# Weight splits, norm vectors and product order in the mixers of a two-block transformer kernel

## The chip, the core and the metric

One core of one Trainium2 chip runs the whole program. Its engines, as the profile names them: PE (TensorE, matmul; PEld is its weight load), DVE (VectorE), ACT (ScalarE), POOL (GpSimd) and SP (SyncE), which issues the DMAs. The metric is device microseconds of one execution, as the median of several runs. Times in a trace count from the first instruction of the span.

## What is computed

Input x is 256 tokens of 1024 channels in float32. A first block (an even layer with two kinds of attention, an odd layer with retention, a final norm) is followed by a second block, and the change is in the first half of that second block, the mixers. Cut to that half:

```python
def first_block(x, ...):          # even_layer, odd_layer, then:
    return rms_norm(x, final_norm)

def second_block(h, ...):
    hn = rms_norm_2(h, g_pre_mix)
    u, q, k, v = split(hn @ w_in)                     # 512, 512, 128, 128 columns
    y_ssm = s5_mixer(u, ...)                          # state space, gelu, gated product with w_glu
    y_attn = sliding_window_sink_attention(rotary(q), rotary(k), v, sinks)   # 8 heads, window 128
    merged = concat([rms_norm_2(y_ssm, g_ssm_out), rms_norm_2(y_attn, g_attn_out)])
    h = h + rms_norm_2(merged @ w_out, g_post_mix)
    hn = rms_norm_2(h, g_pre_ffn)
    ff = (silu(hn @ w_gate) * (hn @ w_up)) @ w_down
    return h + rms_norm_2(ff, g_post_ffn)
```

## The kernel before

Tokens lie in two tiles of 128 partitions, `x[0]` and `x[1]`. Large products are made in float32r out of two parts of each operand: high part times high part, high times low and low times high (`mm_xs`, `proj_xs`, `proj_tmajor`, lines 268 to 336). The class `Weights` (lines 46 to 90) streams the weights: `load` (L63) issues a DMA of 512 KB on SP into one of five raw buffers; `_prepare` makes the high part with a cast on ACT (L73) and the low part with a subtraction (L78), on DVE or, for one tile in `SH[part]`, on POOL. The list at L36 gives the mixers one tile in 2 and the feed-forward one in 8. `next` prepares two tiles ahead of use, in six buffers. The mixers have 22 tiles of [128, 1024]: u 4, q 4, kv 2, glu 4, output 8.

The order of instructions on each engine is fixed when the program is built: a planner simulates the engines and takes what is ready first; `tc.high_priority()` moves a block ahead of others, and a manual dependency (`hold`, `behind`) puts one instruction behind another. At run time each engine takes its list in order, and SP its list of DMAs.

The stages of the mixers and what the change touches in them:

- Norms (L812 to L839): x times (g_pre_mix times g_final) on DVE (L224), then transposed on PE (L235), copied by ACT (L242) and subtracted by DVE (L243) into the two parts of xT. The factors of a token come in after the products: POOL multiplies x by g_final (L827), ACT squares (L202), DVE scales x (L837).
- u, q and kv products (`proj_xs`), each scaled by ACT on its way out of PSUM (L863, L876, L889; v by DVE, L890). The rotary embedding of q and k: six small POOL operations per call (L847 to L852); k is then doubled by DVE (L892) and transposed (L895).
- State space (L900 to L940): two halves `b`, each of two quarters `hf`. A quarter is 16 products with its tables into PSUM (L912), then on DVE two multiplications (L918, L919), two sums (L920, L921), two scans (L924), a multiplication by the cosines (L927) beside one by the sines on POOL (L928), two sums into X (L930, L931), and 12 products into bank `py` (L934 to L936), 64 columns wide: quarter 0 fills the partitions 0 to 63 of the bank, quarter 1 the others. Each is two PE records. Then a gelu on ACT (L938), transposes (L946) and a split (L326, L327).
- The tables of quarters 1 and 3 are loaded into buffers that earlier quarters used (L796, L797): the y table of a later quarter waits for an earlier quarter's products.
- Attention (L966 to L990): in pairs of heads, scores (L338), masked minimum (L346, L348), minimum with the sink (L970), exponentials on ACT (L355, L356, L973), the sum and its reciprocal (L974, L976), scaling (L977, L978), transposes (L362), copies (L364), p times v (L372) into the one `py` bank, squares (L985, added up on POOL, L987), and the two parts with the gain (L988, L989).
- POOL also makes x times g_pre_ffn (L993) and g_pre_ffn times g_post_mix (L994).
- The gated product of the state space (`zp`): DVE adds the biases (L1004, L1006), ACT the tanh, POOL multiplies by g_ssm_out (L1007), DVE makes the gated value (L1008), transposed into its two parts, and the same without the gain (L1010) for the norm's factor.
- Output: first the products of the state space's half (scaled by ACT, L1047), then those of attention's half; DVE joins them (L1064), ACT squares, DVE multiplies by the two gains (L1069) and adds x (L1074); transposes; POOL multiplies by g_post_mix (L1078) and DVE updates x (L1079). Then the feed-forward's first products start.

The line of the split before:

```python
i = nc.scalar.copy(h[:, :n], r[:, :n])                                                            # L73
self.lows.append(eng.tensor_tensor(lo[:, :n], r[:, :n], h[:, :n].bitcast(F32), op=ALU.subtract))  # L78
```

## Time and profile before

| | us |
|---|---|
| median of 3 runs | 811.92 |
| lowest, highest | 810.0, 812.02 |
| span of the profiled execution | 810.7 |
| PE busy | 780.7 (96%) |
| DVE busy | 560.7 (69%) |
| ACT busy | 408.3 (50%) |
| POOL busy | 237.2 (29%) |

The span runs from the first to the last instruction of one execution; the median of the runs is 1.2 us above it. A busy time is the union of an engine's instructions. PE's instructions overlap, so a row of PE can be busy without being at its peak rate. In a timeline a row gives start, duration, engine, line, operation, the tiles it writes and reads, the shape, how many were merged, and in brackets how long the engine was idle before it and what ended that.

### The profile page before, as it was taken

To read this page: it belongs to the slowest core of one execution; us is meant where nothing else is said; L and a number is where in the kernel's file an instruction comes from. 1 tells how busy PE (TensorE), PEld (TensorE's weight loads), DVE (VectorE), ACT (ScalarE), POOL (GpSimd) and SP (SyncE) were. 2 spreads that over 40 slices of the span, in tenths; PEclk is the share of its full clock that TensorE was granted. 3 is DMA by queue.
4 is the path that set the end of the run, shared out by engine and by line. 5 is a ranking of instruction groups with operands and counts; after the bars stand their busy time and mean duration, and the time that the engine had idled before them with its cause. 6 is when DMAs were issued, how large, how long until landed. Compare 5 with 4: busy or idle time off the path is not lost.

```text
span 810.7 us, 13533 instructions
## 1 busy us (share of the span) xinstructions
PE 780.7 (96%) x5114; PEld 682.1 (84%) x5114; DVE 560.7 (69%) x1013; ACT 408.3 (50%) x680; POOL 237.2 (29%) x274
## 2 busy tenths in 40 slices
PE   7989999999999999999999999989798999999996
PEld 5978997998997789898989887876577999999886
DVE  6987668678778468585766757698849856565433
ACT  5766565457455355344444355736645544443331
POOL 4662111013604212120202006853653322221110
PEclk9999999999999999999999999999999999999999
DMA  7687544644744757453636494852243765555431
GB/s 284 222 270 234 172 165 131 208 150 154 238 161 133 234 186 254 154 188 124 208 119 194 151 334 152 301 195 85 81 127 110 235 200 177 189 183 181 156 130 53
DMA packets 47427, 146.46 MB, mean 181 GB/s; under 512 B 5361, under 2 KB 11777, under 8 KB 47362
## 3 DMA queue, kind: packets, MB, share of 16 engines
q1 hardware_dynamic: 47362, 145.60, 54.5%
q8 instruction: 40, 0.66, 0.3%
q14 instruction: 25, 0.20, 0.1%
HBM read 137.70 MB, written 7.88 MB: 180 GB/s over the span
## 4 chain that ended last, share of the span: by engine, by line
PE 82%; DVE 5%; POOL 4%; issue 3%; ACT 3%; DMA 3%; SPq 0%; POOLq 0%; DVEq 0%; ACTq 0%
PE bpp L274 12%; PE bpp L275 12%; PE bpp L278 12%; PE bpp L251 9%; PE bpp L250 9%; PE bpp L252 9%; PE bat L252 3%; PE bat L251 3%; PE bat L250 3%; PE bpy L372 2%; PE bat L338 2%; PE bpt L362 1%; PE bpp L289 1%; DVE wl L78 1%; POOL wl L78 1%
## 5 line engine op out<-in xcount | busy, mean ns | idle before, releaser
L78 DVE TENSOR_TENSOR wl<-wraw,wh 128x1024 fp32r<-128x1024 f32 x211 | 276.5, 1321 | 114.9 <-ACT wh L73 114.9
L73 ACT CAST wh<-wraw 128x1024 fp32r<-128x1024 f32 (+1 forms) x233 | 238.6, 1045 | 190.0 <-PE bpp L251 54.1
L251 PE MATMUL bpp<-xTl,wh 128*128 128x256 f32 (+1 forms) x680 | 193.3, 284 | 0.0
L250 PE MATMUL bpp<-xTh,wh 128*128 128x256 f32 (+1 forms) x680 | 193.1, 284 | 0.0
L252 PE MATMUL bpp<-xTh,wl 128*128 128x256 f32 (+1 forms) x680 | 192.9, 284 | 0.0
L251 PEld LDWEIGHTS bpp<-xTl,wh 128*128 128x128 f32 (+1 forms) x680 | 127.3, 187 | 2.6 <-issue 1.9
L250 PEld LDWEIGHTS bpp<-xTh,wh 128*128 128x128 f32 (+1 forms) x680 | 127.3, 187 | 1.8 <-issue 1.3
L252 PEld LDWEIGHTS bpp<-xTh,wl 128*128 128x128 f32 (+1 forms) x680 | 127.3, 187 | 1.0 <-issue 0.8
L274 PE MATMUL bpp<-wh,xTh 128*128 128x512 f32 (+1 forms) x288 | 110.9, 391 | 0.8 <-ACT xTh L242 0.8
L275 PE MATMUL bpp<-wl,xTh 128*128 128x512 f32 (+1 forms) x288 | 109.6, 385 | 0.0
L78 POOL TENSOR_TENSOR wl<-wraw,wh 128x1024 fp32r<-128x1024 f32 x22 | 57.7, 2624 | 62.9 <-ACT wh L73 62.9
L278 PE MATMUL bpp<-wh,xTl 128*128 128x512 f32 (+1 forms) x288 | 74.2, 382 | 0.0
L274 PEld LDWEIGHTS bpp<-wh,xTh 128*128 128x128 f32 x288 | 54.5, 190 | 13.3 <-ACT xTh L242 1.7
L275 PEld LDWEIGHTS bpp<-wl,xTh 128*128 128x128 f32 x288 | 54.5, 189 | 11.1 <-DVE wl L78 0.6
L278 PEld LDWEIGHTS bpp<-wh,xTl 128*128 128x128 f32 x288 | 52.2, 188 | 11.1
L274 PE MATMUL bpp<-wh,yh 128*128 128x512 f32 x128 | 50.5, 400 | 0.0
L275 PE MATMUL bpp<-wl,yh 128*128 128x512 f32 x128 | 50.4, 396 | 0.0
L252 PE MATMUL bat<-xTh,wl 128*128 128x256 f32 x160 | 45.1, 282 | 0.0
L250 PE MATMUL bat<-xTh,wh 128*128 128x256 f32 x160 | 45.1, 282 | 0.0
L251 PE MATMUL bat<-xTl,wh 128*128 128x256 f32 x160 | 45.0, 281 | 0.0
L1119 POOL TENSOR_TENSOR gr<-gr,Rh 128x512 f32<-128x512 f32 x10 | 14.3, 1427 | 75.5 <-ACT th L1118 75.5
L278 PE MATMUL bpp<-wh,yl 128*128 128x512 f32 x128 | 35.6, 395 | 0.0
(380 smaller groups left out, 1312.3 us busy)
## 6 DMA issues: line engine op xcount, KB each, us to landing
wraw<-in_w_o SPq DMA_DIRECT2D x40, 512.0 KB, 4.3
wraw<-in_w_gate SPq DMA_DIRECT2D x22, 512.0 KB, 3.8
wraw<-in_w_up SPq DMA_DIRECT2D x22, 512.0 KB, 4.2
wraw<-in_w_dn SPq DMA_DIRECT2D x22, 512.0 KB, 3.7
wraw<-in_w_v SPq DMA_DIRECT2D x16, 512.0 KB, 4.6
wraw<-in_w_g SPq DMA_DIRECT2D x16, 512.0 KB, 4.4
wraw<-in_w_q SPq DMA_DIRECT2D x12, 512.0 KB, 4.1
wraw<-in_w_va SPq DMA_DIRECT2D x8, 512.0 KB, 6.6
```

The source lines that it names most:

```text
L73: i = nc.scalar.copy(h[:, :n], r[:, :n])
L78: self.lows.append(eng.tensor_tensor(lo[:, :n], r[:, :n], h[:, :n].bitcast(F32), op=ALU.subtract))
L250: T.matmul(ps, lh, rh, start=first, stop=False)
L251: T.matmul(ps, lh, rl, start=False, stop=False)
L252: T.matmul(ps, ll, rh, start=False, stop=last)
L274: T.matmul(ps, lh[:, k0 + k, st], wh, start=first and k == 0, stop=False)
L275: T.matmul(ps, lh[:, k0 + k, st], wl, start=False, stop=False)
L278: T.matmul(ps, ll[:, k0 + k, st], wh, start=False, stop=last and k == n - 1)
L289: m = T.matmul(ps[t], xp[:, k, st], tiles[k // 2][0][:, 512 * (k % 2):512 * (k % 2) + 512], start=xp is xTh and k == 0, stop=False)
L338: i = T.matmul(ps[j][:, o], q[rows, qs], k[rows, ks], start=True, stop=True)
L372: i = T.matmul(o[64 * j:64 * j + 64], v[:, b, vc], src, start=b == 0, stop=b == 1)
L1119: G.tensor_tensor(two(gr), two(gr), rep2(Rh), op=ALU.mult)
```

## The change

- No large operation of the mixers on POOL: `SH[2]` goes from 2 to 0, so DVE makes all 22 low parts; the sine product of the state space goes to DVE; the products by g_final, g_ssm_out, g_pre_ffn and g_post_mix leave POOL.
- Norm vectors in the weights: w_u3, w_q3, w_kv3 and w_o3 are multiplied by the norm's gain while they are split. A tile is then split in 2 blocks of 512 columns (kv: 4 of 256), each with an ACT activation scaled by a column of gains and a DVE `scalar_tensor_tensor`. Three small DMAs on SP bring the gains at the start of the program, in program order after the load of x[0] and ahead of the first weights.
- x is transposed without a gain; x is scaled by both factors in one DVE operation.
- The products into `py` are issued in pairs, one of each quarter, for both quarters after their X.
- The rotary embedding takes three POOL operations per call, k is doubled by ACT's broadcast read, v is scaled by ACT; the sink goes into the masked minimum as its starting value.
- The weights of attention's output half are planned, and its products made, before those of the state space's half.
- After the output products DVE multiplies by g_post_mix, updates x, then multiplies by g_pre_ffn.

```diff
-SH = (0, 0, 2, 8)
+SH = (0, 0, 0, 8)
...
+        g = self.gains[len(self.done)]
+        if g is not None:
+            m = g.shape[1]
+            for b in range(m):
+                sl = slice(b * n // m, (b + 1) * n // m)
+                i = nc.scalar.activation(h[:, sl], r[:, sl], AF.Copy, scale=g[:, b:b + 1])
+                if self.after:
+                    self.tc.add_manual_dep(i.ins, self.after[0].ins.name, NOSYNC, reason="order")
+                self.lows.append(nc.vector.scalar_tensor_tensor(lo[:, sl], r[:, sl], g[:, b:b + 1], h[:, sl].bitcast(F32),
+                                                                op0=ALU.mult, op1=ALU.subtract))
...
+    def gain_cols(name):
+        g = const.tile([P, 8], F32, name="gc_" + name)
+        nc.sync.dma_start(g, a[name])
+        return g
+
+    g_pm, g_fc, g_mo = (gain_cols(n) for n in ("g_pre_mix", "final_cols", "g_mix_out"))
+    V.tensor_tensor(g_pm, g_pm, g_fc, op=ALU.mult)
     for n in ("w_u3", "w_q3", "w_kv3"):
-        w.plan(xs(n, 0), SH[2])
+        w.plan(xs(n, 0), SH[2], g_pm)
...
-    for sl in (slice(0, 2), slice(2, 4)):
+    for i in (1, 0):
         for c in range(2):
-            w.plan(xs("w_o3", c)[sl], SH[2])
+            w.plan(xs("w_o3", c)[2 * i:2 * i + 2], SH[2], g_mo[:, 4 * i:4 * i + 4])
...
-        G.tensor_tensor(g_pm, g_pm, g_fin, op=ALU.mult)
-        last = [gained_transposed(t, halves(g_pm), KB[t]) for t in range(2)]
+        last = [transposed([x[t][:, :512], x[t][:, 512:]], 8, xTh, xTl, 0, t, KB[t]) for t in range(2)]
...
-            G.tensor_tensor(xc, xc, g_fin[:, h * 512:(h + 1) * 512], op=ALU.mult)
...
+        V.scalar_tensor_tensor(x[t], x[t], r1, g_fin, op0=ALU.mult, op1=ALU.mult)
...
-            A.mul(kd[:, :, 0, :], kv_, r2s[t][0])
-            V.tensor_scalar(v[:, t, :], ps[t][:, P:S], r2s[t][0], None, op0=ALU.mult)
-            rotary(kd[:, :, 0, :], kd[:, :, 0, :], t, 2)
-            V.tensor_copy(kd[:, :, 1, :], kd[:, :, 0, :])
+            A.mul(kd, ps[t][:, :P].rearrange("p (a b) -> p a b", a=2)[:, :, None].to_broadcast([P, 2, 2, 64]), r2s[t][0])
+            A.mul(v[:, t, :], ps[t][:, P:S], r2s[t][0])
+            rotary(kd.rearrange("p a b c -> p (a b) c"), t, 4)
...
-                G.tensor_tensor(bs, z, sn, op=ALU.mult)
+                V.tensor_tensor(bs, z, sn, op=ALU.mult)
...
-                for s in range(4):
-                    o = py[64 * hf:64 * hf + 64, s * P:(s + 1) * P]
-                    T.matmul(o, U[:, 4 * qi + s, :], tb(qy, QT0, s), start=True, stop=False)
-                    T.matmul(o, X[:, 0, s, :], tb(qy, QHR, s), start=False, stop=False)
-                    T.matmul(o, X[:, 1, s, :], tb(qy, QHI, s), start=False, stop=True)
+                Xs.append(X)
+
+            for s in range(4):
+                for n in range(3):
+                    for hf in range(2):
+                        qi = 2 * hf + b
+                        lhs = U[:, 4 * qi + s, :] if n == 0 else Xs[hf][:, n - 1, s, :]
+                        T.matmul(py[64 * hf:64 * hf + 64, s * P:(s + 1) * P], lhs, tb(qts[qi][1], (QT0, QHR, QHI)[n], s),
+                                 start=n == 0, stop=n == 2)
...
-        s, nm = masked_min(b3, sc[h % 2], band[:, :P], band[:, P:])
-        V.tensor_scalar(nm, nm, nsinks[:, h:h + 1], None, op0=ALU.min)
+        s, nm = masked_min(b3, sc[h % 2], band[:, :P], band[:, P:], nsinks[:, h:h + 1])
...
-            A.activation(mah[:, j, :], po[:, :S], AF.Copy, scale=g_att[:, j:j + 1])
-            V.scalar_tensor_tensor(mal[:, j, :], po[:, :S], g_att[:, j:j + 1], mah[:, j, :].bitcast(F32),
-                                   op0=ALU.mult, op1=ALU.subtract)
-
-    for t in range(2):
-        G.tensor_tensor(xg[t], x[t], g_ff, op=ALU.mult)
-    G.tensor_tensor(g_ff, g_ff, g_post, op=ALU.mult)
+            split(mah[:, j, :], mal[:, j, :], po[:, :S])
...
-            G.tensor_tensor(zg, zb, g_ssm, op=ALU.mult)
-            V.scalar_tensor_tensor(zg, zz, 1.0, zg, op0=ALU.add, op1=ALU.mult)
-            transposed([zg], 4, mh, ml, 0, t, ["at"])
             V.scalar_tensor_tensor(zz, zz, 1.0, zb, op0=ALU.add, op1=ALU.mult)
+            transposed([zz], 4, mh, ml, 0, t, ["at"])
...
     woa = [[w.next(), w.next()] for c in range(2)]
     for t in range(2):
         for c in range(2):
+            pb = bank("pp")
+            mm_xs(pb, mah, mal, 0, t, woa[c], 4, 512, True, True)
+            A.mul(oa[t][c], pb, r_att[t])
+    pa = [[], []]
+    wos = [[w.next(), w.next()] for c in range(2)]
+    for t in range(2):
+        for c in range(2):
             pa[t].append(bank("pp"))
-            mm_xs(pa[t][c], mah, mal, 0, t, woa[c], 4, 512, True, True)
+            mm_xs(pa[t][c], mh, ml, 0, t, wos[c], 4, 512, True, True)
...
             for c in range(2):
+                sl = slice(c * 512, (c + 1) * 512)
+                o, xc = oa[t][c], x[t][:, sl]
+                m = V.tensor_tensor(o, o, g_post[:, sl], op=ALU.mult)
+                V.scalar_tensor_tensor(xc, o, r, xc, op0=ALU.mult, op1=ALU.add)
                 xn.append(nrm.tile([P, 512], F32, tag="xn", bufs=3, name="xn"))
-                V.scalar_tensor_tensor(xn[c], pg[c], r, xg[t][:, c * 512:(c + 1) * 512], op0=ALU.mult, op1=ALU.add)
+                V.tensor_tensor(xn[c], xc, g_ff[:, sl], op=ALU.mult)
...
-            G.tensor_tensor(oa[t][c], oa[t][c], g_post[:, sl], op=ALU.mult)
-            V.scalar_tensor_tensor(x[t][:, sl], oa[t][c], r, x[t][:, sl], op0=ALU.mult, op1=ALU.add)
```

## Rows read from the trace of the kernel before

**Rows 1.** The page's first part: busy time, share and instruction count of each engine.

```profile
PE 780.7 (96%) x5114; PEld 682.1 (84%) x5114; DVE 560.7 (69%) x1013; ACT 408.3 (50%) x680; POOL 237.2 (29%) x274
```

**Rows 2.** Busy time of each engine by stage (us from the span's start): u, q and kv products; state space; attention with the gated product; output products; the step to the feed-forward. Columns: stretch, its length, busy of PE, PEld, DVE, ACT and POOL (instructions), granted clock, DMA share, GB/s.

```profile
496.00:534.00 38.00, 38.00 (x233) 32.44 (x232) 30.29 (x36) 25.64 (x41) 31.89 (x33) 1.00 0.65 230
534.00:557.00 23.00, 18.81 (x144) 14.70 (x142) 20.91 (x60) 11.91 (x27) 8.93 (x12) 1.00 0.43 155
557.00:592.00 35.00, 28.30 (x150) 20.34 (x148) 27.94 (x63) 21.55 (x59) 19.11 (x12) 0.95 0.31 105
592.00:609.00 17.00, 16.95 (x75) 13.66 (x76) 8.35 (x11) 6.49 (x10) 9.48 (x7) 1.00 0.37 110
609.00:618.00 9.00, 5.27 (x36) 4.22 (x35) 9.00 (x14) 5.63 (x12) 5.46 (x4) 1.00 0.07 29
```

**Rows 3.** Timeline of POOL from 478 to 620 us: its large operations of the mixers.

```profile
500.24 2.40 POOL L78 TENSOR_TENSOR wl<-wraw,wh 128x1024 fp32r<-128x1024 f32 x1
...
535.75 2.52 POOL L78 TENSOR_TENSOR wl<-wraw,wh 128x1024 fp32r<-128x1024 f32 x1
...
562.27 4.73 POOL L993 TENSOR_TENSOR xg<-x,g_ff 128x1024 f32<-128x1024 f32 x2 [9.28 <-DMA g_ff<-in_g_pre_ffn]
567.08 2.53 POOL L994 TENSOR_TENSOR g_ff<-g_ff,g_post 128x1024 f32<-128x1024 f32 x1
574.76 1.30 POOL L1007 TENSOR_TENSOR zg<-zb,gain_g_ssm_out 128x512 f32<-128x512 f32 x1 [5.15 <-DVE zb L1006]
576.01 2.39 POOL L78 TENSOR_TENSOR wl<-wraw,wh 128x1024 fp32r<-128x1024 f32 x1
...
582.27 2.37 POOL L78 TENSOR_TENSOR wl<-wraw,wh 128x1024 fp32r<-128x1024 f32 x1
```

**Rows 4.** Timeline of DVE over the same stretch.

```profile
500.44 3.29 DVE L78 TENSOR_TENSOR wl<-wraw,wh 128x1024 fp32r<-128x1024 f32 x1
...
525.99 0.68 DVE L918 TENSOR_TENSOR sb<-bat,qt 128x512 f32<-128x512 f32 x1
...
531.45 1.69 DVE L927 TENSOR_TENSOR sb<-sz,qt 128x512 f32<-128x512 f32 x1
...
534.59 1.48 DVE L931 TENSOR_TENSOR X<-sb,sb 128x252 f32<-128x252 f32 x1
535.99 2.36 DVE L892 COPY kd<-kd 128x128 f32<-128x128 f32 x1
...
541.50 1.21 DVE L78 TENSOR_TENSOR wl<-wraw,wh 128x1024 fp32r<-128x1024 f32 x1
...
544.08 0.19 DVE L892 COPY kd<-kd 128x128 f32<-128x128 f32 x1
...
553.36 0.42 DVE L931 TENSOR_TENSOR X<-sb,sb 128x252 f32<-128x252 f32 x1
...
562.38 2.29 DVE L974 TENSOR_TENSOR dn<-dn,es 128x2 f32<-128x2 f32 x1
...
565.11 1.97 DVE L977 TENSOR_SCALAR s<-s,rd 128x128 f32<-128x128 f32 x1
...
568.38 1.39 DVE L970 TENSOR_SCALAR nm<-nm,nsinks 128x2 f32<-128x2 f32 x2
...
576.09 2.87 DVE L1008 SCALAR_TENSOR_TENSOR zg<-zb,zg 128x512 f32<-128x512 f32 x1 [1.41 <-POOL zg L1007]
...
582.86 2.87 DVE L78 TENSOR_TENSOR wl<-wraw,wh 128x1024 fp32r<-128x1024 f32 x1
...
586.25 0.47 DVE L989 SCALAR_TENSOR_TENSOR xTl<-bpy,g_att,xTh 128x256 fp32r<-128x256 f32 x1
...
591.55 0.48 DVE L989 SCALAR_TENSOR_TENSOR xTl<-bpy,g_att,xTh 128x256 fp32r<-128x256 f32 x1 [0.94 <-ACT xTh L988]
...
602.75 2.13 DVE L1069 TENSOR_TENSOR pg<-oa,g_ff 128x512 f32<-128x512 f32 x1
...
609.02 0.75 DVE L1079 SCALAR_TENSOR_TENSOR x<-oa,rstd_po,x 128x512 f32<-128x512 f32 x1
```

**Rows 5.** Timeline of ACT: an exponential of attention and its wait; a cast of a weight tile; an activation of 512 columns scaled by a column.

```profile
569.73 0.41 ACT L355 ACTIVATE s<-s,nm 128x128 f32<-128x128 f32 x1 [6.75 <-DVE nm L970]
...
597.44 1.05 ACT L73 CAST wh<-wraw 128x1024 fp32r<-128x1024 f32 x1 [5.45 <-PE bpp L278]
598.40 0.68 ACT L1047 ACTIVATE oa<-bpp,rstd_ys 128x512 f32<-128x512 f32 x1
```

**Rows 6.** Timeline of PE: products into the y bank one after another, a pair of heads' products side by side, products of the state space's output half, and the step to the feed-forward.

```profile
555.62 0.38 PE L935 MATMUL bpy<-qy,X 128*64 128x128 f32 x2
555.84 0.38 PE L936 MATMUL bpy<-qy,X 128*64 128x128 f32 x2
...
583.26 0.79 PE L274 MATMUL bpp<-wh,xTh 128*128 128x512 f32 x1
...
589.79 0.87 PE L372 MATMUL bpy<-pT,v 128*64 128x256 f32 x8
...
611.77 0.39 PE L274 MATMUL bat<-wh,xTh 128*128 128x256 f32 x1 [1.74 <-ACT xTh L242]
```

**Rows 7.** The chain that ended last, its first microseconds: start, us, what.

```profile
1.53 0.42 SPq L131
...
2.00 6.25 DMA wraw<-in_w_va
```

More of the change, by code (lines that the diff above doesn't have):

```diff
@@ L51, in __init__, with plan @@
         self.after, self.loaded, self.loads, self.lows = [], [], 0, []
-        self.jobs, self.shares, self.done, self.used = [], [], [], 0
-    def plan(self, aps, share=0):
+        self.jobs, self.shares, self.gains, self.done, self.used = [], [], [], [], 0
+    def plan(self, aps, share=0, gain=None):
         self.jobs += aps
         self.shares += [share] * len(aps)
+        n = gain.shape[1] // len(aps) if gain is not None else 0
+        self.gains += [gain[:, n * j:n * j + n] if n else None for j in range(len(aps))]
     def load(self):
@@ L85, in behind @@
     def behind(self, i):
-        for lo in self.lows[self.used:]:
+        for lo in self.lows[-self.ahead:]:
             self.tc.add_manual_dep(lo.ins, i.ins.name, NOSYNC, reason="order")
@@ L956, in model_kernel @@
     nc.sync.dma_start(g_ff, a["g_pre_ffn"].partition_broadcast(P))
-    xg = [lt.tile([P, D], F32, name=f"xg{t}") for t in range(2)]
-    g_ssm = gain_tile("g_ssm_out")[:, :512]
     bglu = gain_tile("b_glu")
-    g_att = bw.tile([P, 4], F32, name="g_att")
-    nc.sync.dma_start(g_att, a["g_attn_out"])
     sqs = bw.tile([P, S], F32, name="sqs")
@@ L1001, in model_kernel @@
         with tc.high_priority():
-            zb, zz = (b2.tile([P, 512], F32, tag="po", bufs=5, name="zb") for _ in range(2))
-            zg = nrm.tile([P, 512], F32, tag="xn", bufs=3, name="zg")
+            zb, zz = (lt.tile([P, 512], F32, tag="po", bufs=8, name="zb") for _ in range(2))
             V.tensor_tensor(zz, zp[t][1], bglu[:, 512:], op=ALU.add)
@@ L1038, in post_norm_add @@
                         nc.sync.dma_start(out[t * P:(t + 1) * P, sl], x[t][:, sl])
-    oa = [[b2.tile([P, 512], F32, tag="po", bufs=5, name="oa") for c in range(2)] for t in range(2)]
-    wos = [[w.next(), w.next()] for c in range(2)]
-    for t in range(2):
-        for c in range(2):
-            pb = bank("pp")
-            mm_xs(pb, mh, ml, 0, t, wos[c], 4, 512, True, True)
-            A.mul(oa[t][c], pb, r_ssm[t])
+    oa = [[lt.tile([P, 512], F32, tag="po", bufs=8, name="oa") for c in range(2)] for t in range(2)]
     pss = bank("py")
@@ L1182, in _layout @@
     a["positions"] = c(np.asarray(i["positions_2"], np.int32)[0][ORDER].reshape(2, P).T)
[L1183 removed]
+    for n in ("g_post_mix", "g_pre_ffn", "g_post_ffn", "b_glu"):
         a[n] = c(i[n + "_2"][0])
[L1185 to L1186 removed]
     a["sinks"] = c(i["attn_sinks_2"][0])
```

77 lines of the change are left out of this document (32 added, 45 removed).

## The prediction

> **What bounds the kernel now.** I read the page first. PE is busy for 96% of the span and DVE for 69% [rows 1], so PE sets the time wherever it is full, and the question is where it is not. The table by stage answers that: through the u, q and kv products PE has no idle time at all, and then come three stages with holes. In the state space PE is busy 18.81 of 23 us, in attention with the gated product 28.30 of 35, in the step to the feed-forward 5.27 of 9 [rows 2]. That is 4.2 + 6.7 + 3.7 = 14.6 us of idle PE, all of it in the mixers. In the same stages DVE is busy 20.91 of 23, 27.94 of 35 and 9.00 of 9 [rows 2]. So in the holes DVE is what PE waits for.
>
> Then I read the timelines of DVE and POOL side by side, to see what fills DVE. A low part of a weight tile takes DVE 1.21 us when POOL is still (the one at 541.50) [rows 4]. The one that starts at 500.44 takes 3.29: POOL began a 2.40 us subtraction at 500.24 [rows 3, 4], and the DVE one ends 1.1 us after POOL's end at 502.64. It waited for POOL's instruction to end and then did its own work. The same shows at 562 to 570, where POOL runs three products of 1024 columns in a row (4.73 and 2.53 us) [rows 3]: a DVE addition of 2 columns lasts 2.29, a scaling of 128 columns 1.97, two minima of 2 columns 1.39 [rows 4]. These are steps of attention, and the next exponential on ACT starts at 569.73 after 6.75 us of waiting for that minimum [rows 5]. So a good part of DVE's busy time is time in which it stands behind a POOL instruction, and attention stands behind DVE.
>
> **State space (to the last X, 553.36 + 0.42 = 553.8).** Lost to POOL there: 1.69 - 0.68 for the cosine product, 1.48 - 0.42 for a sum into X, 2.36 - 0.19 for the copy that doubles k, together 4.2 us [rows 4]; the plain durations are those of the other instances or of an equal shape [rows 4]. The copies themselves go (2 x 0.19). Added to DVE: four sine products of 512 columns at 0.68 = 2.7, and the low part that POOL made at 535.75 [rows 3], 1.2. Net -0.7 us, which is the near bound. The far bound is a DVE that does nothing but the state space from 525.99 on: a quarter is 4 operations of 512 columns at 0.68 and two scans that I price like them, and 4 sums at 0.42, so 5.8 us, four quarters 23, the end at 549 and 4.6 us gained. I take -2.5, between them: the doubled k no longer waits on DVE, so scores can start earlier, but the low parts still have to go somewhere.
>
> The y products: 96 records 0.11 us apart (two rows of two, 0.22 apart) [rows 6], 10.6 us of PE. In pairs they should take half: a pair of heads' eight records of 256 and 128 columns, issued the same way, take 0.87 us in all [rows 6], where one after another they would take 4 x 0.22 + 4 x 0.11 = 1.3. I book 0 on the path all the same. PE is waiting for X when it has these to do, and after the last X 24 pairs at 0.11 remain, 2.6 us, where now 24 single records remain, the same 2.6. If the pairs didn't overlap, it would cost 2.6 us. The later y tables now wait for both quarters' products, where one table could be loaded after the first quarter; I book 0 for that, since the products of the first half now end close to the second quarter's X, and up to 1 us if the tables land late.
>
> **Attention (553.8 to the last low part, 591.55 + 0.48 = 592.0).** What goes: at 562 to 570, 2.29 to about 0.2, 1.97 to at most 0.42, and the 1.39 of the minima, which move into the masked minimum: 5.0 us. The POOL product with g_ssm_out: DVE waits 1.41 for it and its own 2.87 goes too: 4.3. A low part at 582.86 that stands behind POOL: 2.87 - 1.21 = 1.7. The second token tile's gated product: at least the 0.75 of its form. Together 11.7 [rows 3, 4]. What comes: POOL's low parts of 576.01 and 582.27 go to DVE as two blocks each, 2 x 2 x 0.75 = 3.0, and two tiles of DVE's own change from 1.21 to 1.5, 0.6 [rows 3, 4]. Net -8.1. On ACT a gained tile is two activations of about 0.68 for one cast of 1.05 [rows 5], 0.3 us a tile, beside other work.
>
> The price of a gained block is the row of a `scalar_tensor_tensor` on two float32 tiles with a column, 0.75 for 512 columns, against 0.68 for a plain product [rows 4]. Here a rule speaks against the change: the Trainium skill (Vector Engine (DVE) Microarchitecture Reference, Points that are easy to get wrong) says that this form with two SBUF sources that aren't bf16 runs at half throughput. The row does not show that; what it would do is among the rivals.
>
> Then the order of the output products. Now the first token tile's 24 products of the state space's half stand on PE ahead of the last pair's p times v: the bank it needs is free at 586.25 + 0.47 = 586.7 [rows 4], those products run from 583.26, and it starts at 589.79 [rows 6]. With attention's half first nothing of that kind is ahead of it: -3.1. So attention ends 8.1 + 3.1 = 11.2 us sooner relative to the last X, and 13.7 in all, at 578.3. Bounds: 0 if DVE's freed time is used up by other work, and 11.7 + 3.1 = 14.8. PE has room for it: 18.81 + 28.30 busy in the two stages, less the 6.5 of products that move behind (583.26 to 589.79) and 5.3 saved in y, leaves 35 us of work in the 44 us that remain [rows 2, 6].
>
> The price of the new order: those 24 products now run while attention is unfinished, and afterwards cannot. At the rate of the stage after it, 16.95 us for 75 records [rows 2], that is 24 x 0.226 = 5.4 us added behind attention. Products therefore end 13.7 - 5.4 = 8.3 us sooner.
>
> **Step to the feed-forward.** Lost to POOL now: a product of 512 columns lasts 2.13 in the first tile's chain, 1.4 too long [rows 4], and PE waits 1.74 for its first transposed tile [rows 6]. Added: x is updated before it is multiplied by g_pre_ffn, one product of 0.68 more behind the norm's factor. DVE's count is otherwise equal. I take -1.5, with bounds +1 (the longer chain alone) and -3.7 (all of PE's idle time [rows 2]).
>
> **Start.** SP issues one DMA per 0.42 us, and the chain that ended last starts with exactly these issues and the landing of the first weights [rows 7]. Three more issues ahead of them: +1.3, with bounds 0 (if they are issued later) and +2.5. Everything else (the rotary embedding, the norm's factors, the transposes without a gain) lies in the stage in which PE is never idle [rows 2], and is booked at 0: full PE hides it; if the new split fell behind PE there, u, q and kv would each lose about one split, 1.5 us.
>
> **Sum.** -2.5 - 11.2 + 5.4 - 1.5 + 1.3 = -8.5. The profiled execution has a span of 810.7 and the median lies 1.2 above it; the gain is taken off both, so 802.2 for the span and 803.4 for the median.
>
> **Rivals.**
> 1. PE becomes the only bound. DVE is freed so far that PE has no hole left: its 14.6 us of idle time and half of the y products, 5.3, go: 811.9 - 19.9 + 1.3 = 793.3. For it: most of the idle time was traced to POOL above. Against: attention stays a chain through DVE, ACT and PE.
> 2. Attention first starves PE (slower). If attention's last low part doesn't come at least 5.4 us sooner, the state space's products are missing as filler, and PE idles. The place is PE behind the last p times v. If DVE's new work (four sine products, six low parts) takes back most and attention gains 3 us in all: 811.9 - 3 + 5.4 + 1.3 = 815.6. It decides at 586.6: later than that, the order loses.
> 3. It evens out: DVE gives attention 6 us, the order takes 5.4 and the start 1.3, the step gains 0.5: 812.1. For it: DVE is 80 to 90% busy in both stages [rows 2], and the order fixed beforehand may spend the freed time on low parts.
> 4. The gained blocks run at half throughput: 16 blocks of the output tiles at 1.36 instead of 0.75 add 9.8 us to DVE: 813.2. The 0.75 row speaks against it.
> 5. The y products don't overlap: the forecast plus 2.6, 806.0; the heads' row speaks against it.
>
> A clock risk is in the range: the granted clock averages 0.95 in the attention stage, so part of that stage ran at the lower of its two levels (1.2 GHz, not 2.4) [rows 2]; 0.05 x 35 us doubled is 3.5 us at the lower level, and what PE had to do there took twice its time. Fewer y records make PE emptier in the state space; I put one more such stretch at 1 to 2 us.
>
> **How the numbers follow.** Chances: forecast 0.58, rival 1 0.17, rival 2 0.09, rival 3 0.11, rival 4 0.02, rival 5 0.03. A difference under 0.3% (2.4 us) can't be told from none here. Forecast, rivals 1 and 5 are faster by more (0.78), and part of rival 3 (0.03) too: 0.81. Rival 3's rest, rival 4 and the edge of the forecast: 0.10 same. Rival 2: 0.09 slower. The forecast's own bounds, each term at its nearer end for about half of them, are 797 to 808. The range takes in rival 1's 793 nearly and rival 3's 812: 794 to 812.
>
> **What would show it.** Right: DVE low parts near 1.2 us or in blocks of 0.75 throughout the mixers; no DVE instruction of 2 columns above 0.3; y records in pairs 0.11 apart; the exponential's wait of 6.75 gone; attention's last low part before 581; PE without a hole between attention and the last output product; the first PE product 1 to 1.5 us later. Wrong: an attention end after 586.6, holes of PE behind the last p times v, gained blocks above 1 us, a DVE that is full through both stages, or a second stretch at half clock.

## The result and the profile after

The change made the kernel slower: 818.0 us median (817.5 to 824.6, 4 runs) against 811.2 (810.0 to 812.0, 4 runs) of the kernel before, ratio 1.010 [1.006, 1.014] (ratios here are close to those of the means, not of the medians). The forecast was 803.4, with a range of 794 to 812. The profiled executions have spans of 815.8 and 810.7.

The page's first part, as [rows 1]; then the stages of [rows 2], each 3.77 us later, since the kernel after is that late at 500 us (columns: stretch, length, busy us of PE, PEld, DVE, ACT, POOL, granted clock, DMA share, GB/s):

```profile
PE 784.7 (96%) x5114; PEld 687.0 (84%) x5114; DVE 548.4 (67%) x1033; ACT 414.2 (51%) x704; POOL 167.4 (21%) x235
```

```profile
499.77:537.77 38.00, 37.69 (x235) 32.49 (x234) 27.86 (x48) 32.51 (x62) 9.50 (x17) 1.00 0.68 234
537.77:560.77 23.00, 13.60 (x85) 11.11 (x85) 20.26 (x54) 7.04 (x19) 0.29 (x2) 0.70 0.32 115
560.77:595.77 35.00, 34.66 (x209) 25.84 (x210) 21.90 (x72) 23.61 (x66) 3.32 (x5) 0.95 0.28 91
595.77:612.77 17.00, 14.76 (x61) 11.94 (x60) 7.88 (x13) 8.25 (x14) 4.99 (x4) 0.90 0.38 123
612.77:621.77 9.00, 6.34 (x41) 5.01 (x40) 8.55 (x14) 6.50 (x15) 0.87 (x1) 1.00 0.00 0
```

Read against [rows 2], attention looks as hoped: PE idle 0.3 us in place of 6.7, DVE 6 us less busy. Part of what fills PE there is late work, though: the second half's products into `py` end at 565.94, inside this stage. And the state space has 9.4 us of idle PE in place of 4.2, and there the granted clock averages 0.70: 0.30 x 23 x 2 = 13.8 us at 1.2 GHz, against none before. The holes didn't go, they moved: 15.0 us in these five stages, 14.7 before. PE's longest waits in the state space are 4.28 us for the first X, 2.40 and 1.23 for tables that a DMA brings. Lines of PE's timeline, and of DVE's:

```profile
59.02 1.65 PE L361 MATMUL bat<-k,q 64*128 64x128 f32 x8 [5.44 <-DVE nm L371]
...
541.74 0.69 PE L951 MATMUL bpy<-qy,X 128*64 128x128 f32 x2 [4.28 <-DVE X L942]
544.83 3.65 PE L924 MATMUL bat<-U,qt 128*128 128x64 f32 x16 [2.40 <-DMA qt<-w_dram]
...
558.85 0.41 PE L951 MATMUL bpy<-qy,U 128*64 128x128 f32 x2 [1.23 <-DMA qy<-y_dram]
...
565.00 0.27 PE L951 MATMUL bpy<-qy,X 128*64 128x128 f32 x1
565.01 0.38 PE L951 MATMUL bpy<-qy,U 128*64 128x128 f32 x2
```

```profile
555.55 0.41 DVE L943 TENSOR_TENSOR X<-sb,sb 128x252 f32<-128x252 f32 x1
...
570.24 0.16 DVE L984 TENSOR_TENSOR dn<-dn,es 128x2 f32<-128x2 f32 x1 [1.29 <-ACT es L983]
...
583.21 0.75 DVE L84 SCALAR_TENSOR_TENSOR wl<-wraw,gc_g_mix_out,wh 128x512 fp32r<-128x512 f32 x1 [0.36 <-ACT wh L81]
...
592.01 0.42 DVE L350 TENSOR_TENSOR xTl<-bpy,xTh 128x256 fp32r<-128x256 f32 x1 [0.86 <-ACT xTh L349]
```

A two-column addition takes 0.16 in place of the 2.29 of [rows 4], a gained block 0.75, not 1.36. Products of the two quarters start side by side (565.00 and 565.01). The last low part of attention is at 592.01, no sooner than before (591.55); with the 3.77 us taken off it is 3.3 sooner. And the first line shows a hole where nothing was expected, in the even layer at 59 us; the kernel before waits 1.82 us for the same product:

```profile
56.16 0.93 PE L338 MATMUL bat<-k,q 64*128 64x128 f32 x8 [1.82 <-DVE nm L348]
```

To place losses, each PE product is matched with the same one of the kernel before (same tiles and shape, same occurrence); its start less that of before is the shift. For the kernel after the median shift is -0.5 us up to 50 us, 3.1 at 90 to 100, 3.8 at 490 to 506 and 5.1 from 640 on. So in this execution 3.8 us arise ahead of the mixers and 1.3 in them. Where a time is said to be measured from 500 us on, the run's own shift at 490 to 506 is taken off it.

### The profile page after: what moved, and what is told of

Its sections match the earlier page's. It is cut to its first block, busy times and chain, and to the rows that moved or that the text cites. A ratio compares the mean times of both kernels' runs of the same rounds, so it can differ in the third digit from the quotient of the medians.

```text
span 815.8 us, 13520 instructions
## 1 busy us (share of the span) xinstructions
PE 784.7 (96%) x5114; PEld 687.0 (84%) x5114; DVE 548.4 (67%) x1033; ACT 414.2 (51%) x704; POOL 167.4 (21%) x235
## 4 chain that ended last, share of the span: by engine, by line
PE 86%; DVE 5%; DMA 3%; issue 2%; ACT 1%; POOL 1%; SPq 1%; POOLq 0%; DVEq 0%; ACTq 0%
PE bpp L297 13%; PE bpp L298 13%; PE bpp L301 13%; PE bpp L273 9%; PE bpp L275 9%; PE bpp L274 9%; PE bat L273 3%; PE bat L275 3%; PE bat L274 3%; PE bat L361 2%; PE bpy L395 2%; PE bpt L385 2%; DVE wl L94 1%; PE bpy L951 1%; PE bpt L258 1%
## 5 line engine op out<-in xcount | busy, mean ns | idle before, releaser
L94 DVE TENSOR_TENSOR wl<-wraw,wh 128x1024 fp32r<-128x1024 f32 x204 | 254.9, 1262 | 115.2 <-ACT wh L89 115.1
L89 ACT CAST wh<-wraw 128x1024 fp32r<-128x1024 f32 (+1 forms) x215 | 220.9, 1044 | 187.7 <-PE bpp L274 54.0
L301 PEld LDWEIGHTS bpp<-wh,xTl 128*128 128x128 f32 x288 | 52.0, 188 | 11.3 <-issue 0.3
L94 POOL TENSOR_TENSOR wl<-wraw,wh 128x1024 fp32r<-128x1024 f32 x11 | 27.6, 2510 | 56.7 <-ACT wh L89 56.7
L378 ACT ACTIVATE s<-s,nm 128x128 f32<-128x128 f32 x40 | 16.1, 402 | 39.5 <-DVE nm L369 39.3
```

Source lines behind the costliest of these rows:

```text
L301: T.matmul(ps, ll[:, k0 + k, st], wh, start=False, stop=last and k == n - 1)
L378: A.activation(p[:, :P], s[:, :P], AF.Exp, bias=nm[:, 0:1], scale=-1.0, accum_out=dn[:, 0:1])
```

## The experiments

The table gathers all runs (base B: the kernel before, with medians of 812.4 to 813.8 beside these runs; base N: B without large GpSimd operations in the mixers, below; base A: the kernel after). "Start" is the shift at 90 to 100 us, "mixers" the shift at 650 to 700 us less that at 490 to 506, both from the one profiled execution against that of B. The expectations number their theories: 1, the pairs wait for the later y tables; 3, the loads at the start; 4, the order of the output products; 5, u is late behind ACT; 6, DVE stands behind POOL.

| run | edit | median us (range) | ratio to B, 95% | start | mixers |
|---|---|---|---|---|---|
| after | | 818.0 (817.5-824.6) | 1.006-1.014 | 3.1 | 1.3 |
| e1 | A, y products per quarter | 823.0 (814.7-824.9) | 1.007-1.014 | 9.5 | -0.2 |
| e2 | A, y tables resident | 820.8 (814.0-823.1) | 1.006-1.013 | 8.7 | -2.3 |
| e3 | A, gain loads late | 815.9 (812.6-818.7) | 1.002-1.006 | -1.5 | 1.8 |
| e4 | A, state space's half first | 820.3 (811.2-822.2) | 1.003-1.009 | 1.5 | -3.0 |
| e5 | A, norms side by side | 824.5 (822.5-826.9) | 1.013-1.017 | 9.5 | 0.6 |
| e6 | A, rotary table on DVE | 820.4 (817.6-821.5) | 1.007-1.011 | 6.4 | -1.9 |
| e7 | A with e1, e3, e4 | 812.1 (808.0-815.3) | 0.998-1.001 | 3.2 | -1.6 |
| e8 = N | B, GpSimd's large ones on DVE | 802.7 (801.4-803.0) | 0.986-0.990 | -2.1 | -9.4 |
| f1 | N, pairs | 805.3 (803.9-806.7) | 0.989-0.993 | -2.0 | -7.3 |
| f2 | N, attention's half first | 804.6 (801.9-806.0) | 0.988-0.992 | -1.4 | -7.0 |
| f3 | N, u, q, kv gains folded | 808.4 (806.9-809.8) | 0.993-0.997 | -1.4 | -2.9 |
| f4 | N, three loads at the start | 811.6 (808.5-813.1) | 0.996-1.000 | 6.6 | -7.5 |
| g1 | A without those four | 808.8 (805.8-811.6) | 0.993-0.998 | -2.2 | -4.8 |
| g2 | g1, norms side by side | 806.1 (803.9-807.2) | 0.990-0.994 | 0.1 | -9.0 |
| g3 | N, pairs, tables resident | 806.8 (804.4-807.1) | 0.991-0.995 | -0.5 | -5.6 |
| g4 | N, tables resident | 807.8 (805.7-810.7) | 0.993-0.997 | -1.6 | -3.7 |
| h1 | f4, decay tables on DVE | 810.4 (809.9-811.0) | 0.995-0.997 | 4.7 | -7.5 |
| h2 | N, decay tables, gates on DVE | 801.9 (801.1-802.3) | 0.984-0.987 | -2.4 | -8.3 |

The last two columns vary by themselves. In A, e1, e2, e4 and e5 every engine has the same instructions in the same order for the first 100 us, and the start's shift goes from 1.5 to 9.5; in B, N, f1, f2, g3 and g4, with one order too, from -2.1 to 0. In A and e6 the mixers have one order, and their shifts are 1.3 and -1.9. So the start's column tells the two orders apart, but differences of some 3 us in the mixers' column show little alone.

**Parts taken out of the kernel after (e1 to e7).** The edits of e1, e2, e3 and e4:

```diff
 # e1
+                    T.matmul(o, U[:, 4 * qi + s, :], tb(qy, QT0, s), start=True, stop=False)
...
-            for s in range(4):
-                for n in range(3):
-                    for hf in range(2):
 # e2
-                  qtp.tile(YT, F32, tag="qy", name="qy"))
+                  qtp.tile(YT, F32, tag="qy", bufs=4, name="qy"))
 # e3: ahead of the odd layer
+    for g, n in ((g_pm, "g_pre_mix"), (g_fc, "final_cols"), (g_mo, "g_mix_out")):
+        nc.sync.dma_start(g, a[n])
 # e4
-    for i in (1, 0):
+    for i in (0, 1):
```

> The kernel after, with one thing put back: the y products of a quarter follow its own X again, one after another (48 of them per bank, no pairs), so that the first later y table can be loaded after the first quarter's products and not after both. Theory 1 (the pairs make both later y tables wait for all products of the first half; the last y product of the kernel after ends at 565.93, though the last X is there at 555.96): the issues of the two later y tables, at 554.48 in the kernel after, part again, the first before 545; the last y product ends by 561 and the time falls by 4 to 8 us, to 810 to 814. Rival (the state space is late because u and its transposed copies are late, behind gained splits on ACT): the tables move, but the time stays within 2 us of the kernel after, 816 to 820. Second rival (giving up the pairs costs PE 2.6 to 5 us that the tables' earlier landing doesn't return): 818 to 822.

> The kernel after, with the y tables of all four quarters in tiles of their own (four buffers in place of two; two scratch tiles of DVE, the sine products and the scans, get one buffer in place of two to make room). The pairs stay. So no y table waits for a product. Theory 1 (the wait for the tables is the loss): the gap of PE ahead of the second half's y products goes (y products end within 4 us of the last X), the time falls by 5 to 9 us, to 809 to 813, as low as with the products per quarter or lower. Rival (u late, or the clock's fall decides): 815 to 819, although the tables are there.

> The kernel after, but the three small loads of gain columns and their product stand ahead of the odd layer's gain load, some 250 us later, and not at the start. Theory 3 (these three issues at the start, and the new plan of the even layer that they bring about, cost the 3.2 us by which the kernel after is behind from 60 us on): PE's wait ahead of the first attention falls from 5.4 back to about 1.8 us, and the time falls by 2.5 to 4 us, to 814 to 815.5. Rival (the 3.2 us come from the plan as such, or from the new tables of the rotary embedding, not from these loads): 817 to 819.5, or any other shift of the same size.

> The kernel after, with the state space's half of the output product first and attention's half added behind it, as in the kernel before (the factor of the state space goes in first, that of attention in the sum). Theory 4 (the 24 products of the state space's half are worth more as filler while attention is unfinished, 5.4 us, than attention loses by standing behind them, 3.1 us): 814.5 to 816.5. Rival (attention is the chain that ends last, its product first is right): 820 to 823. Third view (both even out, the tables decide): 817 to 819.5.

Theory 1 missed in e1 and e2: the time didn't fall (the interval of the ratio is about A's), and the start, which the edits don't touch, came some 6 us later in both profiles. In the mixers alone the shifts are 1.5 and 3.5 us below A's, where 4 to 9 us of time were expected. e3 gained 2.1 us by the medians, a little less than theory 3 expected. e4 missed by its median, which isn't below A's; its profile has 4.3 us less in the mixers, but its runs spread over 11 us. What they had in common was the start, with shifts of 1.5 to 9.5 us for the same early code. So next the suspects of the start and of u, a combination, and the other way round: the kernel before with the one idea of the change.

```diff
 # e5
-        V.scalar_tensor_tensor(x[t], x[t], r1, g_fin, op0=ALU.mult, op1=ALU.mult)
+            V.tensor_tensor(xc, xc, g_fin[:, h * 512:(h + 1) * 512], op=ALU.mult)
 # e6
-            G.tensor_copy(rot[:, j, :, j, :], cs_)
+            V.tensor_copy(rot[:, j, :, j, :], cs_)
 # e8, on the kernel before; likewise g_pm, xc, xg, g_ff, zg, oa
-SH = (0, 0, 2, 8)
+SH = (0, 0, 0, 8)
-                G.tensor_tensor(bs, z, sn, op=ALU.mult)
+                V.tensor_tensor(bs, z, sn, op=ALU.mult)
```

> The kernel after, with the two norms ahead of the mixers side by side again as in the kernel before: x times g_fin without the first norm's factor (two products of 512 columns per token tile, on VectorE), both sums of squares one behind the other, the second factor from both sums, the first factor into x afterwards. Theory 5 (u is late because the second norm's squares wait for the first norm's factor and then stand behind the gained splits on ACT; U's copies end 4.7 us later than before, measured from 500 us on): U's copies end at least 3 us earlier, the last X 2 to 4 us earlier, the time falls by 2 to 4 us. Rival (the splits themselves fill ACT, 16 blocks of 0.63 and 8 of 0.42 us instead of 10 casts of 1.0): U comes at most 1 us earlier and the time stays within 1.5 us.

> The kernel after, with the four small operations that fill the rotary embedding's table (16 columns each, in the even layer) on VectorE instead of GpSimd. Theory 3, as the traces of the first four runs make it: in the kernel after, these four stand on GpSimd between the copy and the zeroing of the second decay table, whose store stands on SP ahead of weight tiles, and each of them can take 0.4 to 5 us while VectorE is busy; so the weights, the forget gates and the first attention come late by an amount that changes from run to run (3.1 us at 100 us in the kernel after, 9.5 and 8.7 in two variants with the same start). Expected: PE's hole ahead of the first attention as in the kernel before (under 2.5 us), the shift at 100 us between -1 and +1, the median falls by 2.5 to 6 us, to 812 to 815.5, the spread of the runs is smaller. Rival (the three gain loads themselves delay the start): the shift stays at 3 us or more.

> The kernel after with three parts back together: the y products per quarter, the gain loads ahead of the odd layer's gain load, the state space's half of the output product first. By the profiles of the single runs (from 500 us to the feed-forward, against the kernel before: after +1.3, products per quarter -0.2, state space first -3.0; shift at 100 us -1.5 with the late loads), if the parts add: -1.5 - 4.5 = 6 us under the kernel before, 805 to 808. Rival (PE is full from 566 to 592 in the kernel after, so the parts buy the same idle time twice): 809 to 812.

> The kernel before, with only its large GpSimd operations of the mixers moved to VectorE (the lower parts of every second tile, the four sine products, the products with g_fin, g_ff, g_post, g_ssm_out and those of the output); nothing else changes, no gain is folded, no order. Theory 6 (VectorE waits for GpSimd's instructions, and that alone holds the mixers back): the forecast's DVE terms, 2.5 us in the state space and up to 8.1 in attention, come: 802 to 808. Rival (the products themselves fill VectorE as much as the waiting did, or PE is the bound once VectorE is free): 809 to 812. Third (VectorE becomes later ahead of u): 813 to 816.

e5 and e6 missed (U's copies, which end at 524.7 in A measured from 500 us on, come at 525.8; the start stays late). ACT's row of U's copies, before and then in A:

```profile
518.89 1.09 ACT L868 COPY U<-bpt 128x512 f32<-128x512 f32 x2
```

```profile
527.37 1.08 ACT L882 COPY U<-bpt 128x512 f32<-128x512 f32 x2
```

e7 only came back to B. e8 hit: 9.8 us by the medians, all of the gain forecast, by the moves to DVE alone. (Of the 11.3 us between the two profiles, 2.1 lie at the start, where both have the same order, and 9.4 in the mixers.) Its stages, 1.95 us ahead of [rows 2]:

```profile
494.05:532.05 38.00, 38.00 (x235) 32.79 (x234) 29.49 (x49) 25.96 (x41) 10.27 (x24) 1.00 0.74 252
532.05:555.05 23.00, 19.05 (x154) 15.57 (x153) 20.47 (x64) 12.57 (x26) 5.51 (x8) 1.00 0.47 160
555.05:590.05 35.00, 32.59 (x176) 24.94 (x175) 25.93 (x73) 23.40 (x65) 9.09 (x7) 1.00 0.29 94
590.05:607.05 17.00, 14.30 (x75) 11.46 (x75) 16.12 (x23) 9.23 (x19) 3.99 (x3) 1.00 0.38 123
607.05:616.05 9.00, 8.76 (x74) 8.53 (x74) 8.60 (x16) 6.16 (x11) 1.10 (x2) 1.00 0.53 177
```

PE is idle for 9.3 us in place of 14.7, at full clock throughout. Only u comes later: its copies end at 521.9, before at 520.0, both measured from 500 us on. From here the question was turned: what do the other parts cost on N, one at a time?

**Parts added to N (f1 to f4).** N and these four ran on different chips, at different times; B took 812.6 us beside both. f1 has the change's pairs, f2 its order of the output products, f3 its fold of the gain for u, q, kv (loads late), f4 only:

```diff
+    for g, n in zip(gc, ("pm_cols", "final_cols", "mo_cols")):
+        nc.sync.dma_start(g, a[n])
+    V.tensor_tensor(gc[0], gc[0], gc[1], op=ALU.mult)
```

> The kernel before without large GpSimd operations in the mixers (802.7 us in the last call), plus one further part of the change: the y products of both quarters in pairs, after both X. Theory 1 (the pairs take from PE the products with which it filled the second quarter's wait for VectorE, and both later y tables wait for all of them): PE's idle time between the first and the last y product grows by 3 us or more, a stretch at the lower clock appears in the state space, the time rises by 2 to 6 us, to 805 to 809. Rival (half the products' time on PE, 5.3 us, is what counts): 798 to 802.

> The kernel before without large GpSimd operations in the mixers (802.7 us), plus attention's half of the output product first, the state space's half added behind it. Theory 4 (the 24 products of the state space's first token tile are missing as filler while attention is unfinished): 804.5 to 808. Rival (attention ends sooner by as much, 3.1 us): 801.5 to 804. The forecast's own view (attention is no longer behind these products, PE full): 798 to 801.

> The kernel before without large GpSimd operations in the mixers (802.7 us), plus the norm's gain folded into the split of the u, q and kv weights (x is transposed without it; the gain columns are loaded ahead of the odd layer's gain, not at the start). Theory 5 (the gained split takes ACT 0.63 us per 512 columns in place of half a cast of 1.05, and u's scaled copies stand behind it): U's copies end 2 to 4 us later, measured from 500 us on, and the time rises by 1.5 to 5 us, to 804 to 808. Rival (four products of 0.68 us leave VectorE's chain ahead of the transposes, PE is full through this stage): 799.5 to 803.

> The kernel before without large GpSimd operations in the mixers (802.7 us), plus only the three small loads of gain columns at the start, ahead of the first weights, and their product on VectorE; nothing uses them. Theory 3 (the loads and the new plan that follows from them make the forget gates' and masks' chain in the even layer late; mean shift at 100 us 6.4 over six profiles with them, -0.1 over four without): shift at 100 us of 2 to 10, the time 805 to 812 with a wider spread than the kernel without them. Rival (their price is the three issues alone, 1.3 us, or nothing): 802 to 804.5.

All four cost, by the medians: 2.6, 1.9, 5.7 and 8.9 us (f2's range overlaps that of N, so its price isn't clear of the spread). For f4, timelines of POOL, then of SP, first f4, then N:

```profile
26.40 4.88 POOL L534 COPY m<-sm_mag 128x256 f32<-128x256 f32 x1 [5.49 <-DMA w_dram<-m]
31.23 1.43 POOL L467 COPY rc<-sm_trig 128x16 f32<-128x16 f32 x1
32.60 1.61 POOL L468 COPY rs<-sm_trig 128x16 f32<-128x16 f32 x1
34.15 0.10 POOL L535 MEMSET m<- 128x4 f32 x1
```

```profile
34.28 0.33 SPq L536 DMA_DIRECT2D w_dram<-m  x1
34.70 0.38 SPq L63 DMA_DIRECT2D wraw<-in_w_qa  x1
```

```profile
24.62 0.48 POOL L530 COPY m<-sm_mag 128x256 f32<-128x256 f32 x1 [4.17 <-DMA w_dram<-m]
25.16 0.11 POOL L531 MEMSET m<- 128x4 f32 x1
...
34.55 5.46 POOL L530 COPY m<-sm_mag 128x256 f32<-128x256 f32 x1 [0.54 <-DMA w_dram<-m]
...
43.19 2.28 POOL L639 COPY c_f<-c_f 16x256 f32<-16x256 f32 x1 [1.20 <-DVE c_f L637]
```

```profile
26.59 0.49 SPq L532 DMA_DIRECT2D w_dram<-m  x1
27.76 0.33 SPq L63 DMA_DIRECT2D wraw<-in_w_qa  x1
```

The second decay table's copy now falls into a stretch in which DVE runs without a pause and takes 4.88 us in place of 0.48; the new plan puts two more copies ahead of its zeroing; its store waits on SP, and the weights behind the store are issued 6.9 us later. It matters which copy is hit: in N the fourth table's takes 5.46 us, at 34.55, with less behind it. For f3, ACT's timeline, f3 and then N (L881 and L863 write u's scaled copies, L219 and L202 are sums of squares):

```profile
502.03 4.41 ACT L81 ACTIVATE wh<-wraw,gc_pm 128x512 fp32r<-128x512 f32 x7
...
508.18 2.74 ACT L881 ACTIVATE us<-bpp,fn 32x512 f32<-32x512 f32 x4
510.95 3.31 ACT L81 ACTIVATE wh<-wraw,gc_pm 128x256 fp32r<-128x256 f32 x8
514.16 0.61 ACT L219 ACTIVATE junk<-x 128x512 bf16<-128x512 f32 x1
...
516.79 2.76 ACT L881 ACTIVATE us<-bpp,fn 32x512 f32<-32x512 f32 x4
...
523.38 1.07 ACT L886 COPY U<-bpt 128x512 f32<-128x512 f32 x2
```

```profile
508.25 0.63 ACT L202 ACTIVATE junk<-x 128x512 bf16<-128x512 f32 x1
...
510.96 2.77 ACT L863 ACTIVATE us<-bpp,fn 32x512 f32<-32x512 f32 x4
...
518.87 1.07 ACT L868 COPY U<-bpt 128x512 f32<-128x512 f32 x2
```

Behind eight gained blocks of 256 columns, 3.31 us, comes the sum that the second token tile's factor needs, at 514.16 in place of 508.25; the second token tile's scaled copies of u start 5.8 us later, 4.8 once the two traces' own shifts at 500 us (-0.9 and -2.0) are taken off. The last X follows: 555.7 in f3, 551.9 in N, measured from 500 us on.

**What was open (g1 to h2).** g1 undoes the four parts in A, g2 is g1 with e5's edit, g3 and g4 are f1 and N with e2's edit (and the gated product's scratch tiles in another pool). h1 is f4 and h2 is N with the decay tables copied and zeroed on DVE; h2 has the copy of the gates there too:

```diff
-            G.tensor_copy(m4, mag4[:, qs, None].to_broadcast([P, 4, 64]))
-            G.memset(m4[:, :, 0:1], 0.0)
+            V.tensor_copy(m4, mag4[:, qs, None].to_broadcast([P, 4, 64]))
+            V.memset(m4[:, :, 0:1], 0.0)
```

> What remains of the change when the four priced parts are taken out of it: the kernel after, with y products per quarter, the state space's half first, u, q and kv weights split without a gain (x times the gain ahead of the transposes, on VectorE), and only the output gains' columns loaded, ahead of the odd layer's gain. It keeps what the change does beside: no large GpSimd operation, the output gains folded into the split, the sinks inside the masked minimum, k written twice by ACT, the rotary embedding on a doubled table, the norms one behind the other, x updated ahead of the feed-forward's gain. The four prices measured alone on the kernel without GpSimd operations (pairs 2.6, order 1.9, folded u, q, kv 5.7, start loads 8.9 us) make 19.1, and the kernel after stands 15.3 above that kernel; so, if prices add, this gives 799 to 800.5. Rival (the prices overlap, the rest is neutral): 801.5 to 804. Second rival (the norms one behind the other make u late here too): 804 to 808.

> The kernel of the run before it in this call with the two norms side by side (products with g_fin without the first factor). If the norms' chain makes u late: U's copies end 2 us earlier or more and the time falls by 1.5 to 4 us. If ACT's load was what made u late in the kernel after (there the parallel norms changed U by -1 to +1 us only): the time is within 1.5 us of it, on either side.

> The kernel before without large GpSimd operations (802.7 us), with the y products in pairs (805.3 us with that alone) and the y tables of all four quarters resident, so that no table waits for a product (the 512-column scratch tiles of the gated product move to the other side of SBUF and two scratch tiles get one buffer, to make room). If the wait for the tables is the price of the pairs: 801.5 to 803.5, as the same kernel without pairs in this call. If PE, emptied during the second quarter's wait, is the price: 804.5 to 806.5, 2 us or more above the one without pairs. If the pairs gain once no table is late: below the one without pairs.

> The kernel before without large GpSimd operations (802.7 us), y products per quarter, with the y tables of all four quarters resident: the base for the kernel with pairs. If a table was late there too (the last y product ends 2.4 us after the last X): 800.5 to 802. If not: 802 to 803.5.

> The kernel with the three loads at the start and without large GpSimd operations (811.6 us), with the four decay tables copied and zeroed on VectorE instead of GpSimd. If the price of the start loads (8.9 us) is the path that its trace shows (GpSimd's copy of the second decay table, 4.9 us while VectorE is busy, then two other copies, then the zeroing; its store at 34.3 on SP instead of 26.6; weight tiles behind it), the stores no longer wait for GpSimd, the shift at 100 us falls from 6.6 to under 2 and the time to 802 to 805. Rival (the loads delay the start by themselves, or the rest of the new plan does): the shift stays above 4, 808 to 812.

> The kernel without large GpSimd operations in the mixers (802.7 us), with the four decay tables and the copy of the cumulated gates ahead of their store made on VectorE too. The copy of the gates took GpSimd 2.3 us there, 0.4 on VectorE at most, and PE waits 1.9 us ahead of the first attention's transposes: 800 to 802.5 if that chain sets the start; 802.5 to 804 if VectorE, 90 to 100% busy from 20 to 50 us, loses as much.

g1 came 0.8 us above its second rival's range, and g2 points to why: by the medians, norms one behind the other cost 2.7 us (U's copies end at 523.5 and 521.9, measured from 500 us on; mixers -4.8 and -9.0; the ranges of the two overlap). With them side by side the rest of the change is neutral in the mixers (-9.0, N -9.4); g2's median stays 3.4 us above N's, and 2.2 of the 2.8 us between their profiles lie at the start.

g4 is 5 us slower than N for a reason of its own (with one scratch buffer in place of two the second product of a quarter comes behind the sums of the quarter before it, and the last X comes 4.3 us later), so only g3 against g4 counts. There pairs cost nothing, 806.8 against 807.8, which is the outcome that g3's expectation gives to the wait for the tables. The traces speak against that wait: PE's hole ahead of the second half's pairs is the same with and without resident tables, and ends with a minimum on DVE that holds a score bank. f1, with the first and last rows of the pairs behind it, and then g3:

```profile
549.35 0.93 PE L338 MATMUL bat<-kT,qT 64*128 64x128 f32 x8 [3.61 <-DVE nm L348]
550.20 0.44 PE L939 MATMUL bpy<-qy,U 128*64 128x128 f32 x4
...
554.10 0.61 PE L939 MATMUL bpy<-qy,X 128*64 128x128 f32 x8
```

```profile
551.82 1.65 PE L338 MATMUL bat<-kT,qT 64*128 64x128 f32 x8 [3.90 <-DVE nm L348]
```

In f1 the second table lands at 550.02, just in time for the pairs at 550.20, behind the score products. So on N the tables aren't what PE waits for. In A they are in part: PE waits 1.23 us for the first one (the row at 558.85), and the second lands at 560.59, 4.6 us after the last X; the products with X start at 561.83, behind transposes that wait for DVE.

What the pairs do cost shows in f1's rows. They start 2.0 us after the last X and take 4.5 us, at a granted clock of 0.62; so the last y product comes 2.3 us later than in N (556.6 and 554.3, measured from 500 us on), although the last X comes 1.8 sooner. In g3 and g4 it comes at 558.4 and 558.6. In the 23 us of the state space pairs raise PE's idle time from 4.0 to 7.2 (f1 on N) and from 4.6 to 7.8 (g3 on g4), and the time at 1.2 GHz from 0 to 10 and from 3 to 13 us. The second pair of runs has this too and no loss of time, so the emptier PE alone doesn't make the price. The late last y product, which only f1 has, fits it, and isn't shown to be its cause.

h1 freed the weights from the store, and yet gained only 1.2 us on f4, within its rival's range; its start is still 4.7 us late. Another small copy, that of the gates ahead of their store, is long now, 6.38 us where N has 2.28:

```profile
44.36 6.38 POOL L643 COPY c_f<-c_f 16x256 f32<-16x256 f32 x1 [4.14 <-DVE sm_fr L509]
```

So the start loads cost some 9 us; that they do it through these copies is read from the traces and not shown. h2, with both copies on DVE and no start loads, has the lowest median: 801.9 us, 0.985 [0.984, 0.987] of B, not clearly below N. The same two moves together with the start loads weren't tried.

## Why the prediction was wrong

The gain was forecast rightly and comes from the part that the forecast named; the losses stood at 0 or nearly so. Two of the forecast's own signs of being wrong came: attention ends after 586.6 (at 592.4), and more stretches run at half clock.

- **DVE behind POOL: right.** Forecast -2.5 in the state space and -8.1 in attention. In N, measured from 500 us on, the last X comes 1.9 us sooner (551.9, before 553.8) and attention's last low part another 6.5, 8.4 in all (583.6, before 592.0). How much of it was waiting behind POOL's instructions, and how much waiting for POOL's results, isn't told apart. Pairs do run side by side and gained blocks take 0.75: rivals 4 and 5 fall.
- **Failed step: "Everything else ... lies in the stage in which PE is never idle, and is booked at 0: full PE hides it."** PE did stay full there (37.69 of 38). But that stage hands over U, and the state space starts with it: measured from 500 us on, U's copies end at 524.7 in A, 521.9 in N and 520.0 before, and in A PE then waits 4.28 us for the first X. Here full PE didn't hide the lateness of what ACT leaves for the next stage. The bound, about one split of 1.5 us for each of u, q and kv, was for splits that fall behind PE, and so missed this. Folded gains cost 5.7 us on N, the serial norms 2.7 between g1 and g2. In A, which has both, they overlap: U is no later than in f3 alone (525.4).
- **Failed step: start "+1.3, with bounds 0 and +2.5".** The issues were costed, and PE's first weight product even came sooner (9.47 us, before 11.07). The new order of the even layer that comes with them was not: 8.9 us on N. f4's trace points to small copies and the weights behind their store; h1 took four of these copies away and got 1.2 us back, so the way it costs stays open.
- **Failed step: "I book 0 on the path all the same" for the pairs.** It counted 24 pairs in 2.6 us right behind the last X, and not that products which had filled PE while DVE worked on the second quarter were gone. In f1 they start 2.0 us late and take 4.5, and the time rises by 2.6 on N (by nothing in g3 against g4). The table wait, for which up to 1 us was set aside, isn't met in f1; in A PE waits 1.23 us for the first table, and the second lands 4.6 us after the last X.
- **Order of the output products: right in sum, in part by luck.** -3.1 + 5.4 = +2.3 forecast, +1.9 measured, within the spread of the runs. But attention's last low part comes only 1.3 us sooner than in N, not 3.1 (582.3 and 583.6, one profile each).
- **The clock** was set at one more stretch of 1 to 2 us; A has 13.8 + 3.5 + 3.4 = 20.7 us at 1.2 GHz in the five stages (before: 3.5), most of it in the state space, where PE is emptiest, and N none. What this cost apart from the holes isn't shown.

The prices, four on N and that of the norms between g1 and g2, add up to 2.6 + 1.9 + 5.7 + 8.9 + 2.7 = 21.8 us; A stands 15.3 above N by the medians, 16.7 with each against the B beside it. They overlap (u late twice), and A's start varies. How much is which overlap stays open. No rival of the forecast names what decided: rival 2, the only slower one, rests on the order, which costs 1.9.

## What to carry to other kernels

When one change bundles several ideas, cost each by what it takes from the next stage: a stage with a full PE need not hide that what it hands on is late, and products moved behind a wait no longer fill it. Measure the main idea alone first; here seven moved operations and one constant gave all of the gain. Small loads or copies put at the start can move a whole plan, so look there for a shift before explaining the stage that was changed.

## What was not expected

The hold between the two engines seems to work both ways. [Rows 3] and [rows 4] show DVE behind POOL's instruction. In the even layer POOL's copies are long while DVE is busy: the copy of 256 columns takes 0.40 us or up to 5.46, the one of the gates 2.28 to 6.38, while no DVE instruction beside it lasts over 1.3 us. The Trainium skill (SBUF — State Buffer, SBUF: two separate sides) says that of a VectorE instruction with two SBUF inputs and a GpSimd one that reads SBUF the one that starts first has the shared ports for the whole instruction, and the other waits. The traces agree with the conflict (the 3.29 us of [rows 4]), but a copy that takes 4.88 us in place of 0.48 is held for longer than any one instruction beside it lasts. Why one copy is held and another isn't, no run here shows: the first one in f4 takes 0.40 us, with DVE running beside it too.
